# A two-branch streaming encoder layer: weight sums moved to VectorE, lag-kernel copies to GpSimd, S5 runs and projection B's loads begun in the last projection pair

## Chip, cores and metric

One core of a Trainium2 chip. The metric is the device time of one launch in microseconds, the median over runs. The engines are called TensorE (PE in the profile), ScalarE (ACT), VectorE (DVE), GpSimd (POOL) and SyncE (SP).

## What is computed

One layer over 2048 prompt frames and 8 x 16 sample frames (2176 in all), model width 1024, all in float32:

```python
h = rmsnorm(x, ln_g)
u_a, z_a, u_b, z_b, g_a, g_b = split(h @ w_in)          # 512, 512, then 4 x 1024 columns
y_a = gelu(s5_mixer(u_a, ...))                          # 32 groups of 16 channels, 64 complex states each
y_a = y_a * sigmoid(y_a @ w_glu + b_glu)
p_a = (y_a * silu(z_a)) @ w_pa
y_b = rglru(causal_conv(u_b, ...), ...)                 # conv of width 4, gated linear recurrence
p_b = (y_b * silu(z_b)) @ w_pb
m   = sigmoid(g_a) * p_a + sigmoid(g_b) * p_b
out = x + m @ w_out                                     # then a final rmsnorm
```

It also returns the last states of the recurrences and of the conv.

## The kernel before

Every matrix product is done with float16 halves: an operand is a high part and a low part, and a product takes three matmuls (`passes`, L161 to L163: high by high, high by low, low by high). Frames go in tiles of 512 columns, the sample frames in one tile of 128.

The program's order on each engine is written by the kernel itself. Stages, in order of time:

- the norm and the S5 input projection; then four blocks of gate columns done directly;
- sixteen *pairs* (`run_pair`): each multiplies two blocks of 128 columns of `w_in` with all frames. A pair is two `quad`s of seven block products, one for frame tiles 0 and 1 and one for 2 and 3 (a Strassen-like scheme), with the sample tile between them: 15 positions, `pos` 1 to 7, 8, and 9 to 15. Pairs alternate between branch B columns ("b") and gate columns. The last pair is of the kind "za";
- projection B: `p_b` tile by tile (n = 0 to 4, eight blocks m each), beside which the S5 runs go;
- the GLU, the projection of branch A and the merge, then the output projection.

**Weights of a pair.** `w_forms` makes the scheme's eight weight forms from the four blocks A11, A12, A21, A22. Four are sums of blocks, each computed by one `gtt` (GpSimd `tensor_tensor`, L56) into `wt` (`t`) or in place into `wraw` (A21). `high` (ScalarE) then makes the float16 high part, `low` (VectorE) the low part. `tt` is the same operation on VectorE (L53). The eight steps run beside the pair before, one a position, and each yields the cost that it charges.

**Background work.** After each product, `hook` calls `pump` with a budget (2.8 less what the position itself costs). `pump` lets `tasks` and then `low` go on until the budget is used up. `tasks` holds the conv and recurrence work of branch B (`b_work`, one task for two tiles) and the S5 runs; `low` holds `w_spill` (44 weight blocks split and written to DRAM, 16 of them for `w_pb`) and two `s5_prep` generators. `busy(NO_SPILL)` and `busy(NO_PREP)` stop these at some places of a pair: `place` is 0 + `pos` in a "b" pair and 15 + `pos` in a gate pair.

**S5.** `s5_prep` makes, for each of the 16 pairs of groups q, an input matrix `wb`, an output matrix `wc` (products on GpSimd, L56) and a kernel of lags. The last one goes through DRAM (`kpD`), comes back as `dd`, and `lags` copies it into another order (`d2`, ScalarE, two activations for a q) and stores it into `sD`. `s5_run(q)` loads `sD[q]` into one of four pages of the tag `t1` (L1415), `u` and `etD`, waits seven clocks, and then takes some six steps on TensorE, ScalarE and VectorE, with temporary tiles from one page `temp`. Four runs at most are in flight. `tail_start` waits for all runs and all spills, then loads `wo` and prepares the GLU's input: `ya` is read back (L1588), split into `yh` (ScalarE and VectorE).

**The last pair.** `hook_z` takes the place of the plain hook. At positions 8 to 11 it loads the four `wpb` pages (tag `t0`, which holds frame sums of the first quad until then), at 9 it calls `s5_open`, at 13 `y_load(0)`, branch B's output of tile 0. `y_load` first pumps until the tile's last block has been handed to its store. All these DMAs go through SyncE's queue, in program order with the loads of spill blocks (L1157) and of `dd` (L1293). The S5 runs are put into `tasks` only after this pair.

Of the kernel before, what the change touches and what calls it, by code (L numbers as in the profile page):

```python
# [8 lines left out]
F32 = mybir.dt.float32  # L9
# [4 lines left out]
MUL, ADD, SUB, MAX, MIN = ALU.mult, ALU.add, ALU.subtract, ALU.max, ALU.min  # L14
# [3 lines left out]
P = 128  # L18
# [29 lines left out]
def build(tc, I, O):  # L48
    nc = tc.nc
    V, S, G, PE, SP = nc.vector, nc.scalar, nc.gpsimd, nc.tensor, nc.sync  # L50

    def tt(out, a, b, op):
        V.tensor_tensor(out=out, in0=a, in1=b, op=op)  # L53

    def gtt(out, a, b, op):
        G.tensor_tensor(out=out, in0=a, in1=b, op=op)  # L56
# [19 lines left out]
    def scopy(out, a, scale=1.0):  # L76
        act(out, a, AF.Copy, scale=scale)

    with ExitStack() as es:
# [108 lines left out]
        pga = es.enter_context(tc.tile_pool(name="pga", bufs=1))  # L188
# [8 lines left out]
        hs = pga.tile([P, KB, 2, P], F16, name="hs")  # L197
# [17 lines left out]
        with ExitStack() as p1x:  # L215
# [328 lines left out]
            for n in range(4):  # L544
# [8 lines left out]
                for m in range(4):  # L553
                    p = proj(lambda k: wua[m][:, k], n)
# [33 lines left out]
                    if n == 3:  # L588
                        SP.dma_start(out=uD[1024 * m:1024 * m + 1024].rearrange("(p t) x -> p (t x)", t=8),
                                     in_=uE[m].rearrange("p t l j c -> p (t l j c)"))  # L590
# [10 lines left out]
        def page_b(tag, shape, name, dt=F16):  # L601
            return pgb.tile([P] + list(shape), dt, tag=tag, name=name, bufs=4)
# [6 lines left out]
        def gt(shape, dt=F32, name="g"):  # L609
            return gp.tile(list(shape), dt, tag="g", name=name, bufs=slots)  # L610
# [49 lines left out]
        tasks = []  # L660
        low = []
        branch_b = True
        clock = 0
# [109 lines left out]
        def w_forms(raw, W):  # L773

            r1, r2 = raw
            A11, A12, A21, A22 = r1[:, 0:4], r1[:, 4:8], r2[:, 0:4], r2[:, 4:8]
            t = wp.tile([P, 4, P], F32, tag="wt", name="wt", bufs=1)
            for h in range(2):
                W[h] = None

            def high(nm, src):
                h, i = FORMS[nm]
                if W[h] is None:
                    W[h] = w_half()
                scopy(W[h][:, i, :, 0], src, WS)

            def low(nm, src):
                h, i = FORMS[nm]
                stt(W[h][:, i, :, 1], src, WS, W[h][:, i, :, 0], MUL, SUB)

            high("A11", A11)
            gtt(t, A21, A22, ADD)
            yield 0.1
            low("A11", A11)
            high("S1", t)
            yield 0.7
            low("S1", t)
            gtt(t, t, A11, SUB)
            high("A12", A12)
            yield 0.7  # L800
            low("A12", A12)
            high("S2", t)
            yield 0.7
            low("S2", t)
            gtt(t, A12, t, SUB)
            yield 0.7
            high("A21", A21)
            high("S4", t)
            yield 0.2
            low("A21", A21)  # L810
            gtt(A21, A11, A21, SUB)
            low("S4", t)
            yield 1.4
            high("S3", A21)
            high("A22", A22)
            yield 0.2
            low("S3", A21)
            low("A22", A22)
            yield 1.3
# [304 lines left out]
        prepared = set()  # L1124

        place = 0

        def busy(no):

            return branch_b and place in no  # L1130

        NO_SPILL = range(13, 22)
        NO_PREP = range(11, 22)

        def w_spill():
# [49 lines left out]


        todo = list(range(16))
        temp = None

        def scratch(nm):  # L1190

            if nm == "w":
                return temp[:, 512:1024].rearrange("p (a r c) -> p a r c", a=2, r=2)
            return temp[:, 1024:1280].rearrange("p (r c) -> p r c", r=2)

        def s5_prep(second):

            def lags(q, dd):
                d2 = gt([P, 2, 4, P], F16, name="d2")
                for j in range(2):  # L1200
                    scopy(d2[:, j].rearrange("p a (h t) -> p a h t", t=8),
                          dd.rearrange("p g l (j t h) -> p j (g l) h t", j=2, t=8)[:, j])
                G.dma_start(out=sD[q, :, 2], in_=d2.rearrange("p j a x -> p (j a x)"))
                prepared.add(q)

            dd = None
            while second and not prepared:
                yield Later(1)
            while todo:
# [4 lines left out]
                q = todo.pop(0)  # L1214
# [30 lines left out]
                p = ps("a", (P, 4, P))  # L1245
# [22 lines left out]
                for g in range(2):  # L1268
# [3 lines left out]
                    for j in range(2):  # L1272
                        w = P - 16 * j
                        PE.matmul(o[:, 16 + P * j:16 + P * j + w], lhsT=lb,
                                  rhs=wc[:, j, g].rearrange("p (h t) -> p t h", t=8)[:, 0:w // 16],
                                  start=True, stop=True)
# [12 lines left out]
                dd = q, gt([P, 2, 2, 256], F16, name="dd")  # L1289
                for g in range(2):  # L1290
                    for l in range(2):
                        kk = kpD[q, g, :, l, 128:384]
                        SP.dma_start(out=dd[1][:, g, l],  # L1293
                                     in_=bass.AP(kk.tensor, kk.offset, [list(kk.ap[0]), [-16, 8], list(kk.ap[1])]))
# [39 lines left out]
        for n in range(NT):  # L1334
            if n == 1:
                load_states()
            for i in range(2):
                direct(2 + i, n, lambda k: W1[2 * i + k // 4][:, k % 4])
                if n < NT - 1:
                    c = next(wg) if n > 1 else 0  # L1340
# [65 lines left out]
        running = 0  # L1406

        def s5_run(q):
            nonlocal running
            while q not in prepared or running > 3:  # L1410
                yield Later(1)
            running += 1
            page = page_b("t1", (2048,), "sp", F32)
            sp, ph = page[:, 0:1536].bitcast(F16).rearrange("p (a x) -> p a x", a=3), page[:, 1536:1792]
            SP.dma_start(out=sp, in_=sD[q])  # L1415
            u = gt([P, 2, 2, 2, NC], F16, name="u")
# [1 line left out]
                         in_=uD[256 * q:256 * q + 256].rearrange("(g p) x -> p g x", g=2))  # L1418
# [4 lines left out]
            dd = sp[:, 2].rearrange("p (j a x) -> p j a x", j=2, a=4)  # L1423
# [9 lines left out]
            n = P  # L1433
            er, ei = (ph[:, o:o + n][:, None, :].to_broadcast([P, 2, n]) for o in (0, P))
            m16_ = m16c[:, q:q + 1].to_broadcast([P, n])
            w, hs_ = scratch("w"), scratch("hs")
            tt(w[:, 0], v[:, :, 0:n], er, MUL)
            tt(w[:, 1], v[:, :, 0:n], ei, MUL)
            tt(hs_[:, 0], w[:, 0, 0], w[:, 1, 1], ADD)
# [28 lines left out]
            for g in range(2):  # L1468
                p = ps("b")[:, 0:272]
                pj = [p[:, 0:NC], p[:, NC:272]]  # L1470
                uf = [u[:, g, b].rearrange("p j c -> p (j c)") for b in range(2)]
                PE.matmul(p, lhsT=dd[:, 0, 2 * g], rhs=uf[0], start=True, stop=False)
                PE.matmul(p, lhsT=dd[:, 0, 2 * g], rhs=uf[1], start=False, stop=False)
                for a, b in pas:
                    PE.matmul(pj[1], lhsT=dd[:, 1, 2 * g + a], rhs=u[:, g, b, 0], start=False, stop=False)
                for j in range(2):
                    for a, b in pas:
                        PE.matmul(pj[j], lhsT=wcs[:, a, j, g], rhs=hst[:, g, b], start=False, stop=False)
                PE.matmul(p, lhsT=dd[:, 0, 2 * g + 1], rhs=uf[0], start=False, stop=True)  # L1479
                sc = 1.0 / (VS * WCS)  # L1480
                act(yo[:, g, 0:256].rearrange("p (n j c) -> p j n c", n=4, j=2),
                    p.rearrange("p (j c) -> p j c", j=2)[:, :, 0:P].rearrange("p j (n c) -> p j n c", n=4),
                    AF.Gelu_apprx_tanh, scale=sc)
                act(yo[:, g, 256:272].rearrange("p (j c) -> p j c", j=2),
                    p.rearrange("p (j c) -> p j c", j=2)[:, :, P:NC], AF.Gelu_apprx_tanh, scale=sc)
                r0 = 256 * q + 128 * g
                G.dma_start(out=yDp[:, r0:r0 + P].rearrange("n p x -> p n x"),
                            in_=yo[:, g, 0:256].rearrange("p (n x) -> p n x", n=4))
                G.dma_start(out=yDs[r0:r0 + P], in_=yo[:, g, 256:272])
                running -= g  # L1490
                yield Step(0.6)


# [62 lines left out]
        def y_load(n):  # L1556
            while (7, n) not in stored:
                beside()
            for h in range(2):
                if n < NT - 1:  # L1560
                    Y[n, h] = page_load(page_a("h", (4, 2, 512), "Y"),
                                        ybD[n, 4 * h:4 * h + 4].rearrange("k p l t -> p k l t"))
                else:
                    Y[n, h] = page_load(hs[:, 4 * h:4 * h + 4], ybS[4 * h:4 * h + 4].rearrange("k p l t -> p k l t"))

        def hook_z(pos, c):
            nonlocal clock
            clock += 1
            pump(2.8 - c)
            if pos == 7:  # L1570
                while done["spill"] < 16:
                    clock += 1
                    pump(1e9)
            if 7 < pos < 12:
                wpb_load()
            if pos == 9:
                s5_open()
            if pos == 13:
                y_load(0)

        run_pair(15, hook_z)
        branch_b = False
        temp = pga.tile([P, 2048], F32, tag="w", name="temp", bufs=3)
        s5_init()
        def ya_load(m, n):
            if n < NT - 1:
# [45 lines left out]
            for _ in chain(glu_prep(0), glu_prep(1)):  # L1632
                yield Step(1.4)

        for q in range(16):
            tasks.append([clock + 3 * q, s5_run(q)])
        tasks.append([clock, tail_start()])

        def load_w(dst, src):
# [20 lines left out]
        for n in range(NT):  # L1660
            w = TILES[n][1]
            for m in range(8):
# [4 lines left out]
                p = ps("mm")[:, :w]  # L1667
# [196 lines left out]
```

## Time and profile before

| | us |
|---|---|
| median of 3 runs (lowest to highest) | 1551.13 (1546.92 to 1555.46) |
| the profiled execution's own time | 1549.53 |
| its span | 1547.7 |
| TensorE busy | 1446.3 (93%) |
| VectorE busy | 1034.2 (67%) |
| ScalarE busy | 815.5 (53%) |
| GpSimd busy | 505.3 (33%) |

The span runs from the first to the last instruction of the profiled execution; the time of that execution is 1.8 us longer. TensorE's busy time counts matmuls that overlap, so it is not time at the peak rate. The sixteen pairs lie between 230.4 and 983.75 us of the span, projection B between 983.75 and 1213.7, the GLU, the projection of branch A and the first output products up to 1284.

### The profile page before, as it was taken

What the parts mean: (1) busy time and instruction counts of PE and PEld (TensorE: products, weight loads), DVE (VectorE), ACT (ScalarE), POOL (GpSimd) and SP (SyncE); (2) the same over time, 40 slices, a digit from 0 to 9 for tenths busy, and PEclk for the clock granted to TensorE, in tenths of its full rate; (3) what the DMA queues carried; (4) which work ended last, traced back from release to release, by engine and by line L of the source; (5) the groups of instructions that cost most, each with busy time, mean ns of one, the idle gap of its engine ahead of it and who ended that gap; (6) DMA issues with size and microseconds to landing.
All of it is one profiled execution on the core that took longest, in us unless ns stands there. A gap on an engine that the chain in (4) does not pass through costs nothing.

```text
span 1547.7 us, 22800 instructions
## 1 busy us (share of the span) xinstructions
PE 1446.3 (93%) x8168; PEld 724.0 (47%) x8168; DVE 1034.2 (67%) x1913; ACT 815.5 (53%) x1526; POOL 505.3 (33%) x781
## 2 busy tenths in 40 slices
PE   7999999999899999998898899799999899999998
PEld 4544445444444444444443444355555544454444
DVE  5546768867588686887768777444445696665543
ACT  7642446757577575874856758423222562542322
POOL 0790133444536444274363642223332200000000
PEclk9999999999999999999999999899999899999999
DMA  8325223332423424241333241998766772163521
GB/s 207 106 92 208 89 77 93 102 122 86 140 82 109 130 86 140 76 158 61 104 127 92 87 134 69 324 360 292 251 214 221 265 255 72 70 219 107 177 82 55
DMA packets 168490, 222.21 MB, mean 144 GB/s; under 512 B 39258, under 2 KB 117738, under 8 KB 166328
## 3 DMA queue, kind: packets, MB, share of 16 engines
q1 hardware_dynamic: 144440, 150.96, 30.8%
q0 software_dynamic: 23936, 69.79, 12.0%
q8 instruction: 64, 1.05, 0.3%
q14 instruction: 50, 0.41, 0.1%
HBM read 133.85 MB, written 86.84 MB: 143 GB/s over the span
## 4 chain that ended last, share of the span: by engine, by line
PE 48%; issue 15%; DVE 11%; POOL 10%; ACT 7%; DMA 7%; SPq 2%; POOLq 0%; DVEq 0%; ACTq 0%
PE ps_mm L161 11%; PE ps_mm L163 11%; PE ps_mm L162 11%; PE ps_mm L1773 4%; PE ps_mm L1771 4%; PE ps_mm L1772 4%; DVE xc L65 2%; POOL wt L56 2%; POOL t L56 2%; POOL wc L56 1%; POOL wb L56 1%; DVE wf L65 1%; ACT L74 1%; POOL wraw L56 1%; ACT d L74 1%
## 5 line engine op out<-in xcount | busy, mean ns | idle before, releaser
L161 PE MATMUL ps_mm<-T,wf 128*128 128x512 f16 x512 | 198.8, 388 | 34.8 <-ACT gs L74 23.0
L163 PE MATMUL ps_mm<-T,wf 128*128 128x512 f16 x512 | 198.7, 388 | 1.3 <-DVE wf L65 1.3
L162 PE MATMUL ps_mm<-T,wf 128*128 128x512 f16 x512 | 198.6, 388 | 0.0
L162 PEld LDWEIGHTS <-wf 128*128 128x128 f16 x1232 | 121.7, 99 | 151.3 <-issue 46.2
L161 PEld LDWEIGHTS <-wf 128*128 128x128 f16 x1232 | 121.8, 99 | 121.6 <-issue 12.0
L163 PEld LDWEIGHTS <-wf 128*128 128x128 f16 x1232 | 121.7, 99 | 119.9 <-issue 7.0
L161 PE MATMUL ps_mm<-h,wf 128*128 128x512 f16 x448 | 171.2, 382 | 2.0 <-ACT wf L74 2.0
L163 PE MATMUL ps_mm<-h,wf 128*128 128x512 f16 x448 | 170.8, 381 | 0.7 <-DVE wf L65 0.7
L162 PE MATMUL ps_mm<-h,wf 128*128 128x512 f16 x448 | 170.8, 381 | 0.0
L161 PE MATMUL ps_mm<-Y,wpb 128*128 128x512 f16 x256 | 98.0, 383 | 11.0 <-DMA Y<-ybD 11.0
L65 DVE SCALAR_TENSOR_TENSOR gb<-gb,ps_mm 128x512 f32<-128x512 f32 (+1 forms) x40 | 24.3, 607 | 115.3 <-PE ps_mm L163 115.3
L1773 PE MATMUL ps_mm<-wo,M 128*128 128x512 f16 (+2 forms) x264 | 98.0, 373 | 3.4 <-DVE M L65 3.4
L1771 PE MATMUL ps_mm<-wo,M 128*128 128x512 f16 (+2 forms) x264 | 98.0, 373 | 0.0
L1772 PE MATMUL ps_mm<-wo,M 128*128 128x512 f16 (+2 forms) x264 | 98.0, 373 | 0.0
L162 PE MATMUL ps_mm<-Y,wpb 128*128 128x512 f16 x256 | 98.0, 383 | 0.0
L163 PE MATMUL ps_mm<-Y,wpb 128*128 128x512 f16 x256 | 97.8, 382 | 0.0
L74 ACT ACT_TABLE_LOAD x64 | 82.1, 1283 | 3.7 <-PE ps_mm L163 1.8
L65 DVE SCALAR_TENSOR_TENSOR xc<-ub,PC,xc 128x512 f32<-128x512 f32 x96 | 79.9, 832 | 3.2 <-ACT xc L74 1.0
L65 DVE SCALAR_TENSOR_TENSOR wf<-wraw,wf 128x512 f16<-128x512 f32 (+1 forms) x82 | 64.8, 806 | 6.2 <-ACT wf L74 6.1
L65 DVE SCALAR_TENSOR_TENSOR xo<-ps_mm,xo 128x512 f32<-128x512 f32 (+2 forms) x35 | 23.6, 674 | 65.4 <-PE ps_mm L1773 65.4
L1065 POOL DMA_DIRECT2D gbD<-gs x40 | 21.8, 546 | 134.4 <-ACT gs L74 134.3
L74 ACT ACTIVATE yo<-ps_a 128x256 f32<-128x256 f32 x64 | 14.7, 281 | 86.1 <-PE ps_a L1479 86.0
(323 smaller groups left out, 3529.2 us busy)
## 6 DMA issues: line engine op xcount, KB each, us to landing
wraw<-w_in SPq DMA_DIRECT2D x38, 512.0 KB, 4.4
sp<-sD SPq DMA_DIRECT2D x16, 768.0 KB, 4.9
xt<-x_prompt SPq DMA_DIRECT2D x16, 512.0 KB, 4.2
gbD<-gs POOLq DMA_DIRECT2D x32, 256.0 KB, 2.3
ybD<-y POOLq DMA_DIRECT2D x32, 256.0 KB, 2.8
gaD<-gs POOLq DMA_DIRECT2D x32, 256.0 KB, 2.5
Y<-ybD SPq DMA_DIRECT2D x8, 1024.0 KB, 9.9
gb<-gbD SPq DMA_DIRECT2D x32, 256.0 KB, 6.9
```

The source lines that it names most:

```text
L56: G.tensor_tensor(out=out, in0=a, in1=b, op=op)
L65: V.scalar_tensor_tensor(out=out, in0=a, scalar=s, in1=b, op0=op0, op1=op1)
L74: S.activation(out=out, in_=a, func=f, **kw)
L161: PE.matmul(p, lhsT=a[:, 0], rhs=b[:, 0], start=first, stop=False, skip_group_check=more)
L162: PE.matmul(p, lhsT=a[:, 0], rhs=b[:, 1], start=False, stop=False, skip_group_check=more)
L163: PE.matmul(p, lhsT=a[:, 1], rhs=b[:, 0], start=False, stop=last, skip_group_check=more)
L1065: G.dma_start(out=dst[m, :, t0:t0 + w], in_=t)
L1771: PE.matmul(p, lhsT=lh[0], rhs=w_[:, 0, c], start=(k == 0), stop=False)
L1772: PE.matmul(p, lhsT=lh[0], rhs=w_[:, 1, c], start=False, stop=False)
L1773: PE.matmul(p, lhsT=lh[1], rhs=w_[:, 0, c], start=False, stop=(k == KB - 1))
```

## The change

Four things are changed.

1. In `w_forms` the four sums go from GpSimd to VectorE, and the yields after them grow by 0.6 each (2.4 in all for a pair).
2. `lags` copies with GpSimd instead of ScalarE.
3. The last pair: `wpb` pages are loaded at positions 2, 3, 5 and 7, `y_load(0)` comes at 8, and the S5 runs are put into `tasks` at position 9 (the first starts two clocks later, the next ones at 3, 5, 7 and then every two clocks). From position 7 on preparation stays stopped (`closing`). The places at which spilling stops change from 13 to 21 to 15 to 20.
4. Runs 4, 5 and 6 take their page from the tag `w` (three pages) and do not count towards the four, so that up to seven are in flight. `temp` is gone, and each run has its own temporary tiles.

```diff
             high("A11", A11)
-            gtt(t, A21, A22, ADD)
-            yield 0.1
+            tt(t, A21, A22, ADD)
+            yield 0.7
...
-            gtt(t, t, A11, SUB)
+            tt(t, t, A11, SUB)
             high("A12", A12)
-            yield 0.7
+            yield 1.3
...
-            gtt(t, A12, t, SUB)
-            yield 0.7
+            tt(t, A12, t, SUB)
+            yield 1.3
...
-            gtt(A21, A11, A21, SUB)
+            tt(A21, A11, A21, SUB)
             low("S4", t)
-            yield 1.4
+            yield 2.0
...
-            return branch_b and place in no
-
-        NO_SPILL = range(13, 22)
+            return branch_b and ((closing and no is NO_PREP) or place in no)
+
+        NO_SPILL = range(15, 21)
...
-                    scopy(d2[:, j].rearrange("p a (h t) -> p a h t", t=8),
-                          dd.rearrange("p g l (j t h) -> p j (g l) h t", j=2, t=8)[:, j])
+                    G.tensor_copy(out=d2[:, j].rearrange("p a (h t) -> p a h t", t=8),
+                                  in_=dd.rearrange("p g l (j t h) -> p j (g l) h t", j=2, t=8)[:, j])
...
-            while q not in prepared or running > 3:
+            other = 4 <= q < 7
+            while q not in prepared or (running > 3 and not other):
                 yield Later(1)
-            running += 1
-            page = page_b("t1", (2048,), "sp", F32)
+            if other:
+                page = pga.tile([P, 2048], F32, tag="w", name="sp", bufs=3)
+            else:
+                running += 1
+                page = page_b("t1", (2048,), "sp", F32)
...
-            w, hs_ = scratch("w"), scratch("hs")
+            w, hs_ = gt([P, 2, 2, P], name="hw"), gt([P, 2, P], name="hs")
...
         def hook_z(pos, c):
-            nonlocal clock
+            nonlocal clock, closing
+            closing = 6 < pos
...
-            if pos == 7:
+            if pos == 2:
                 while done["spill"] < 16:
...
-            if 7 < pos < 12:
+            if pos in (2, 3, 5, 7):
                 wpb_load()
             if pos == 9:
                 s5_open()
-            if pos == 13:
+            if pos == 8:
                 y_load(0)
+            if pos == 9:
+                start = [clock + 2, clock + 3, clock + 5, clock + 7]
+                for q in range(16):
+                    tasks.append([start[q] if q < 4 else start[3] + 2 * (q - 3), s5_run(q)])
...
-        temp = pga.tile([P, 2048], F32, tag="w", name="temp", bufs=3)
...
-        for q in range(16):
-            tasks.append([clock + 3 * q, s5_run(q)])
```

## Rows read from the trace of the kernel before

**Rows 1.** Busy time by engine in the pairs, projection B and the GLU part.

```profile
core 0: us, PE busy (x) PEld busy (x) DVE busy (x) ACT busy (x) POOL busy (x), PEclk, DMA share, GB/s
230.40:983.75 753.35, 701.54 (x3903) 343.64 (x3902) 569.21 (x862) 507.93 (x889) 344.86 (x445) 0.98 0.34 110
983.75:1213.70 229.95, 218.95 (x1542) 124.67 (x1541) 105.04 (x331) 62.26 (x190) 73.46 (x121) 0.98 0.79 272
1213.70:1284.00 70.30, 58.03 (x248) 24.43 (x246) 66.49 (x103) 43.45 (x56) 1.58 (x3) 0.90 0.70 237
```

**Rows 2.** Waits of TensorE in the pairs: total, times, longest, in us.

```profile
PE ps_mm L161 <- ACT gs L74: 23.0, 11, 5.8
PE ps_mm L161 <- ACT ub L74: 10.3, 7, 3.5
PE ps_a L162 <- DVE xs L53: 7.3, 4, 4.3
```

**Rows 3.** Seven half-clock stretches in the pairs, summed; then the two later ones.

```profile
sum 34.12, PE 28.25 PEld 10.36 DVE 19.33 ACT 29.44 POOL 21.25; mean PE 4.04 PEld 1.48 DVE 2.76 ACT 4.21 POOL 3.04
...
987.62:997.86 10.24, 4.55 (x11) 1.62 (x11) 1.75 (x3) 2.14 (x2) 2.35 (x4) 0.50 0.94 319
1216.31:1229.96 13.65, 8.86 (x19) 2.46 (x19) 12.85 (x12) 13.27 (x14) 0.00 (x0) 0.50 0.95 323
```

**Rows 4.** Timeline around 380 to 392 us, GpSimd, ScalarE, TensorE: start, length.

```profile
380.12 1.59 POOL L56 TENSOR_TENSOR wc<-wc,t 128x512 f32<-128x512 f32 x1
...
382.79 1.27 POOL L56 TENSOR_TENSOR wt<-wraw 128x512 f32<-128x512 f32 x1
...
384.10 0.63 ACT L74 ACTIVATE wf<-wt 128x512 f16<-128x512 f32 x1 [4.87 <-POOL wt L56]
...
389.05 2.11 ACT L74 ACTIVATE d<-dd 128x512 f16<-128x512 f16 x2
...
391.70 0.58 PE L161 MATMUL ps_mm<-T,wf 128*128 128x512 f16 x1 [5.83 <-ACT gs L74]
```

**Rows 5.** Waits of ScalarE in the pairs: total, times, longest.

```profile
ACT wf L74 <- POOL wt L56: 48.7, 27, 4.9
```

**Rows 6.** GpSimd in the pairs, slowest and fastest sum: count, busy us, mean ns.

```profile
L56 POOL TENSOR_TENSOR wt<-wt,wraw 128x512 f32<-128x512 f32 x15 | 23.6, 1570 | 26.2 <-DVE wf L65 26.2
...
L56 POOL TENSOR_TENSOR wt<-wraw 128x512 f32<-128x512 f32 x15 | 19.8, 1321 | 14.2 <-DMA wraw<-w_in 14.1
```

**Rows 7.** The widest copy on GpSimd, from the preparation before the pairs.

```profile
L434 POOL COPY pw<-stk x1: 299/299/299, 73.8 to 73.8; 128x64 f32<-128x64 f32 x1
```

**Rows 8.** VectorE by line in the pairs: one operand in PSUM, then both in SBUF.

```profile
L53 DVE TENSOR_TENSOR gs<-ps_mm,gs 128x512 f32<-128x512 f32 x48 | 32.8, 684 | 16.7 <-PE ps_mm L163 16.4
...
L65 DVE SCALAR_TENSOR_TENSOR q<-q,xc 128x512 f32<-128x512 f32 x32 | 28.7, 897 | 0.3 <-ACT q L74 0.2
```

**Rows 9.** Timeline at 714 us, VectorE and GpSimd.

```profile
713.95 5.59 DVE L65 SCALAR_TENSOR_TENSOR xc<-ub,PC,xc 128x512 f32<-128x512 f32 x3
...
714.10 1.25 POOL L56 TENSOR_TENSOR wc<-par 128x256 f32<-128x256 f32 x2
```

**Rows 10.** SyncE's queue around the end of the last pair.

```profile
983.86 2.46 SPq L1293 DMA_DIRECT2D dd<-kpD  x4
986.37 1.14 SPq L1545 DMA_DIRECT2D Y<-ybD  x2
```

**Rows 11.** Waits of TensorE after the pairs.

```profile
PE ps_mm L161 <- DMA Y<-ybD: 11.0, 2, 9.3
PE ps_mm L161 <- ACT yh L74: 4.4, 2, 3.9
```

**Rows 12.** S5 runs' page loads (first and last start), and the GLU input's read-back.

```profile
L1415 SPq DMA_DIRECT2D sp<-sD x16: 319/320/1577, 989.0 to 1162.2; - x16
...
1207.61 10.69 SPq L1588 DMA_DIRECT2D ya<-yDp  x8
```

**Rows 13.** VectorE's low parts of the GLU input, min/median/max ns.

```profile
L53 DVE TENSOR_TENSOR yh<-ya,yh x32: 426/1273/1486, 1216.7 to 1281.5; 128x256 f16<-128x256 f32 x24, 128x64 f16<-128x64 f32 x8
```

More of the change, by code (lines that the diff above doesn't have):

```diff
@@ L1126, in build @@
         place = 0
+        closing = False
         def busy(no):
-            return branch_b and place in no
-        NO_SPILL = range(13, 22)
+            return branch_b and ((closing and no is NO_PREP) or place in no)
+        NO_SPILL = range(15, 21)
         NO_PREP = range(11, 22)
@@ L1187, in build @@
         todo = list(range(16))
[L1188 to L1194, printed above, removed]
         def s5_prep(second):
@@ L1489, in s5_run @@
                 G.dma_start(out=yDs[r0:r0 + P], in_=yo[:, g, 256:272])
-                running -= g
+                running -= 0 if other else g
                 yield Step(0.6)
```

## The prediction

> **What bounds the kernel now.** First the windows by stage, to see whether TensorE is ever short of work [rows 1]. It is the bound nearly everywhere, and what can be won is its idle time and its time at half clock. In the sixteen pairs it is busy 701.5 of 753.4 us, so it is idle 51.8 us. In projection B it is idle 11.0 us, in the GLU part 12.3 of 70.3 us. Then TensorE's waits. In the pairs 33.3 us are waits for a ScalarE eviction (23.0 for the gate snaps, 10.3 for the branch B ones), 7.3 us for VectorE [rows 2]. In B the idle time is one wait, for the first Y tile, 11.0 us [rows 11]. Third the granted clock. It falls to 0.50 (1.2 of 2.4 GHz) behind long waits: in seven stretches of the pairs, 34.1 us in all, with TensorE busy 28.3; once behind the Y wait, 10.2 us, busy 4.6; once in the GLU part, 13.7 us, busy 8.9 [rows 3]. Work at half clock takes twice its time, so half of those busy sums is lost: 14, 2.3 and 4.4 us.
>
> Why ScalarE is late is seen in one timeline [rows 4]. A product for the next PSUM bank waits 5.83 us for a snap. ScalarE had stood 4.87 us for GpSimd's first sum of weights, which was queued on GpSimd behind a product of the S5 preparation (`wc`, begun at 380.12), and it then spent 2.11 us on two lag copies right ahead of that snap. Without these 6.98 us there is no wait. In all, ScalarE waits 48.7 us for such sums in the pairs [rows 5].
>
> **Sums on VectorE.** 15 pairs with four sums, 60 in this stretch. On GpSimd one takes 1.32 to 1.57 us, 60 x 1.45 = 87 us [rows 6]. On VectorE a two-operand operation on 128x512 float32 takes 0.684 us when nothing holds it up [rows 8], so 60 x 0.684 = 41 us are added to 569 busy of 753 (76%) [rows 1]: 81% if nothing is given back. Something is: an operation with both operands in SBUF takes 0.897 us in the mean, one with an operand in PSUM 0.684 [rows 8], and three `xc` steps take 5.59 us while GpSimd works [rows 9]. Bounds for what 87 us of GpSimd work take from VectorE: nothing, and all 87. This form alone loses 32 x 0.213 = 6.8 us, and it is one of many. I take about half of the 87, 40, so the move is neutral for VectorE's sum. What the edit removes is ScalarE's wait, 48.7 us. The grown yields take 15 x 2.4 = 36 units from background work; that work ends in time anyway, since preparation and spill have B as a reserve.
>
> **Lag copies.** 32 copies of 1.05 us (2.11 / 2) leave ScalarE [rows 4], 30 of them in the pairs: 32 us. On GpSimd no copy of this size is in the trace. The bounds are 0.30 us, a copy of 64 columns [rows 7], and 1.57 us, the slowest two-input sum of 512 [rows 6]. It is nearest to the sums in size, so I take 1.3 us: 39 us, less than half of the 87 that leave. What is queued behind a copy there are the store of `sD` and the next `wc` products.
>
> The Trainium skill (SBUF — State Buffer, "Who interferes with whom") says that a VectorE instruction with two SBUF inputs contends with a GpSimd instruction that reads SBUF, and that the second to issue blocks fully. The rows agree (0.897 against 0.684 us, and 5.59 us for three). By that rule the copies, which read SBUF, hold VectorE up as the sums did.
>
> Sum for the pairs: of 33.3 us of eviction waits I take two thirds, 22, and of the 14 us of clock loss 8. Against that, VectorE now makes the sums in order behind `b_work`, and ScalarE can wait there. I charge 8 us, about what it costs today that VectorE is late (7.3) [rows 2]. Net **-22 us**. Bounds: all of the waits and the clock gone, -47; every sum on the path, 60 x 0.684 = +41.
>
> **Y and `wpb` early.** The load of Y is ready to go before the end of the pair, but in SyncE's queue it stands behind four `dd` loads that go at 983.86; Y goes at 986.37 [rows 10]. With preparation stopped there are no `dd` loads ahead of it, and five positions of 753.4 / 16 / 15 = 3.1 us lie between 13 and 8. Ahead of it may still be a spill load that waits for a free tile, and the store of the last `b_work` of tile 0. Wait and clock are 11.0 + 2.3 = 13.3 us; I leave 2: **-11 us** (0 to -13).
>
> **S5 early, seven in flight.** The runs' loads begin at 989.0, the last at 1162.2 [rows 12]: 173 us for 15 steps, four in flight, so four rounds of some 46 us. The GLU's input is read back at 1207.6, with B's end at 1213.7: all of its copies are late. VectorE needs 16 low parts of 1.27 us for the first two tiles, 20 us [rows 13], and is busy 66.5 of 70.3 us there [rows 1]. Now run 0 starts four positions before the pair's end, and three runs of the first seven need no page of the four. Runs 0 to 3, 7 to 10, 11 to 14 and 15 are what queues for the four pages, so the last run begins at 3 x 46 = 138 us after the first instead of 173, and the first some 10 us earlier: the runs end about 45 us earlier. Read-back (10.7 us of issues) and 20 us of copies fit into that. VectorE is busy 105 of 230 us in B and ScalarE 62 [rows 1], so the copies are hidden there; were VectorE as full as in the pairs, those 20 us would come back. Idle time and clock of the GLU part are 12.3 + 4.4 = 16.7 us; I take **-14 us** (0 to -17). The denser runs can make TensorE wait in B now and then: **+2** (0 to 6).
>
> **Sum.** -22 - 11 - 14 + 2 = -45. Against the profiled execution's own 1549.53 us that is 1504.5. The median of the runs is 1.6 us above that execution, so the time is **1506 us**.
>
> **Rivals.**
> - *The lag copies cost VectorE what the sums gave back.* 39 us of GpSimd copies, each holding VectorE for its whole length, put VectorE at 569 + 41 + 39 - 40 = 609 of 753, and ScalarE waits for sums that come late. The pairs then win half: 1506 + 11 = 1517. For it: [rows 9]. Against: half of the ScalarE time is freed whatever VectorE does. Chance 0.18. The rule of the Trainium skill named above is this rival's mechanism.
> - *The S5 runs end early, but the GLU's start does not move.* `tail_start` waits for all spills too, and spills are in `low`, which starves while seven runs use up the budget. Then the 14 us stay: 1520. For it: runs and spills share 2.5 units a clock. Against: after the first seven only four are in flight, as now. Chance 0.14.
> - *Transfers hidden badly.* Spill loads and page waits in SyncE's queue hold Y, and the GLU stays late: only the pairs win, 1506 + 11 + 14 = 1531. Chance 0.09.
> - *VectorE becomes the bound of the pairs (slower).* Place: the positions in which `taps` and `scan` of `b_work` are queued ahead of a sum; ScalarE stands behind it, and the snaps behind ScalarE. Price 0.684 us a sum. It ends above before from the point at which the pairs lose more than the 23 us that the ends win, that is 34 of 60 sums wholly on the path with none of the old waits gone; with all 60 it is 1551 + 41 - 23 = 1569. Against: VectorE has a quarter of its time free. Chance 0.07, and 0.07 more for a loss in the pairs that just eats the 23 us, 1551.
> - *Nearly all idle time goes:* -40 in the pairs, -13, -17: 1481. Chance 0.08.
>
> My forecast has 0.37. Range: from 1484, which leaves the last rival out, to 1536, beyond the third: 0.78 is inside. Half a per cent, 8 us, is about what a measurement of this kernel can tell. Faster by more than that: 0.86 (all but the slower cases); within it 0.07; slower 0.07.
>
> **What will show it.** ScalarE's wait for GpSimd's sums is gone from the pairs, with no wait of like size for VectorE in its place; TensorE's eviction waits there are near 11 us. The half-clock stretches in the pairs are three or fewer. GpSimd's copies show about 1.3 us. Y is issued before 975 us on the old scale, and TensorE goes from the last pair into B without a gap of 3 us. The last S5 page is loaded 45 us earlier, and `yh` is written before the GLU starts. I would be wrong if ScalarE waits for VectorE's sums for more than 25 us, if the copies take over 2.5 us, or if the read-back of the GLU input still stands at the end of B.

## The result and the profile after

The changed kernel takes 1510.37 us (median of four, 1505.42 to 1512.01) against 1551.02 for the kernel before; the ratio is 0.9732, 95% interval 0.9697 to 0.9767. The forecast was 1506 in 1484 to 1536. The profiled execution took 1509.87 us with a span of 1508.1, 39.6 less than before.

Where it came from is not what the sum said. In this table of the two profiles the pairs are counted from the first sample-tile product of the first pair to the last product of the last pair, B from there to its last matmul (with the wait for Y), the GLU part from there to the first output product. The windows of [rows 1] have slightly other ends:

| us | up to the pairs | pairs | B | GLU part | rest | span |
|---|---|---|---|---|---|---|
| before | 237.7 | 745.9 | 230.3 | 61.1 | 272.9 | 1547.7 |
| after | 240.2 | 709.0 | 226.5 | 58.0 | 274.5 | 1508.1 |
| difference | +2.5 | -36.9 | -3.8 | -3.1 | +1.6 | -39.6 |

The windows by stage of the changed kernel, in the columns of [rows 1]:

```profile
232.90:949.30 716.40, 690.70 (x3874) 340.21 (x3873) 567.60 (x911) 475.96 (x851) 265.33 (x385) 0.99 0.36 118
949.30:1175.60 226.30, 221.76 (x1570) 126.49 (x1569) 112.98 (x342) 66.41 (x200) 97.51 (x153) 0.99 0.78 274
1175.60:1242.60 67.00, 56.20 (x247) 24.18 (x245) 66.17 (x103) 42.05 (x55) 1.59 (x3) 0.95 0.69 236
```

TensorE's idle time in the pairs falls from 51.8 to 716.4 - 690.7 = 25.7 us. VectorE's busy time does not move (567.6 against 569.2), though 60 sums were added; which parts of the change add up to that is seen further down. In the GLU part VectorE is as full as before, 66.2 of 67.0 us.

TensorE's waits in the pairs of the changed kernel, to be read against [rows 2]:

```profile
PE ps_a L162 <- DVE xs L53: 7.7, 3, 3.7
PE ps_mm L161 <- DVE gs L53: 7.1, 3, 4.2
PE ps_mm L161 <- ACT gs L74: 4.0, 1, 4.0
...
PE ps_mm L161 <- ACT ub L74: 0.2, 1, 0.2
```

The eviction waits are down from 33.3 to 4.2 us; in their place stand 7.1 us for VectorE's gate sums. The half-clock stretches of the pairs, summed, against the first of [rows 3]:

```profile
sum 17.00, PE 15.39 PEld 5.43 DVE 14.93 ACT 12.92 POOL 2.48; mean PE 3.85 PEld 1.36 DVE 3.73 ACT 3.23 POOL 0.62
```

Four stretches instead of seven, 17 us instead of 34. The prediction wanted three or fewer. ScalarE's wait for the sums in the pairs, against [rows 5], and then GpSimd's lag copy, against the bounds in [rows 6, 7]:

```profile
ACT wf L74 <- DVE wt L53: 19.0, 16, 3.8
```

```profile
L1194 POOL COPY d<-dd x32: 1097/1115/1586, 310.7 to 1118.1; 128x512 f16<-128x512 f16 x32
```

ScalarE waits 19.0 us for VectorE's sums instead of 48.7 for GpSimd's. SyncE's queue before the end of the last pair (949.2), against [rows 10]:

```profile
929.86 2.48 SPq L1286 DMA_DIRECT2D dd<-kpD  x4
...
933.01 0.98 SPq L1542 DMA_DIRECT2D Y<-ybD  x2
```

Y goes 16 us before the pair's end instead of 3 us behind it, and the wait for Y [rows 11] is gone. What is left behind the pairs, TensorE's waits first, then the S5 page loads (first and last start) and the read-back in SyncE's queue, against [rows 12]:

```profile
PE ps_mm L162 <- DVE yh L53: 4.4, 4, 1.3
PE ps_a L1469 <- ACT yo L74: 3.5, 1, 3.5
```

```profile
L1412 SPq DMA_DIRECT2D sp<-sD x16: 319/438/1422, 935.4 to 1121.8; - x16
```

```profile
1167.25 1.49 SPq L1589 DMA_DIRECT2D ya<-yDp  x3
```

The first page load comes 14 us before the pairs' end instead of 5 us behind it, but the last one still 173 us behind it (before: 179), and the read-back still stands at B's end, 8 us ahead of it. That is one of the three signs by which the prediction said it would be wrong, and most of the S5 part of the forecast did not happen.

### The profile page after: what moved, and what is told of

It is laid out like the page before. It is cut to its first block, busy times and chain, and to the rows that moved or that the text cites. A ratio compares the mean times of both kernels' runs of the same rounds, so it can differ in the third digit from the quotient of the medians.

```text
span 1508.1 us, 22745 instructions
## 1 busy us (share of the span) xinstructions
PE 1440.5 (96%) x8168; PEld 725.2 (48%) x8168; DVE 1041.0 (69%) x1977; ACT 786.2 (52%) x1494; POOL 443.4 (29%) x749
## 4 chain that ended last, share of the span: by engine, by line
PE 68%; DVE 13%; issue 7%; ACT 5%; DMA 4%; POOL 2%; SPq 1%; DVEq 0%; POOLq 0%; ACTq 0%
PE ps_mm L161 17%; PE ps_mm L163 17%; PE ps_mm L162 17%; PE ps_mm L1772 4%; PE ps_mm L1771 4%; PE ps_mm L1770 4%; DVE yh L53 2%; DVE wf L65 2%; DVE xc L65 1%; ACT L74 1%; DMA wraw<-w_in 1%; PE ps_a L172 1%; DMA xt<-x_prompt 1%; PE ps_a L1475 1%; PE ps_a L1267 1%
## 5 line engine op out<-in xcount | busy, mean ns | idle before, releaser
L161 PE MATMUL ps_mm<-T,wf 128*128 128x512 f16 x512 | 196.7, 384 | 11.9 <-DVE gs L53 7.1
L163 PE MATMUL ps_mm<-T,wf 128*128 128x512 f16 x512 | 196.5, 384 | 1.5 <-DVE wf L65 1.5
L162 PE MATMUL ps_mm<-T,wf 128*128 128x512 f16 x512 | 196.3, 383 | 0.0
L65 DVE SCALAR_TENSOR_TENSOR xc<-ub,PC,xc 128x512 f32<-128x512 f32 x96 | 74.7, 778 | 2.3
L74 ACT ACTIVATE gs<-ps_mm 128x512 f32<-128x512 f32 (+1 forms) x92 | 48.3, 534 | 29.8 <-PE ps_mm L163 27.1
L1065 POOL DMA_DIRECT2D gbD<-gs x40 | 21.7, 544 | 141.6 <-ACT gs L74 141.6
```

The lines of the kernel that those rows point to most:

```text
L65: V.scalar_tensor_tensor(out=out, in0=a, scalar=s, in1=b, op0=op0, op1=op1)
L74: S.activation(out=out, in_=a, func=f, **kw)
L161: PE.matmul(p, lhsT=a[:, 0], rhs=b[:, 0], start=first, stop=False, skip_group_check=more)
L162: PE.matmul(p, lhsT=a[:, 0], rhs=b[:, 1], start=False, stop=False, skip_group_check=more)
L163: PE.matmul(p, lhsT=a[:, 1], rhs=b[:, 0], start=False, stop=last, skip_group_check=more)
L1065: G.dma_start(out=dst[m, :, t0:t0 + w], in_=t)
```

## The experiments

Profiles of one and the same order of work differ too: through the pairs the changed kernel and three of the kernels below (`e5_front`, `e10_budget`, `e11_four`) hold the same work in the same order but for its very end, and their pairs take 709.0, 714.6, 715.7 and 713.6 us. Differences of pairs under 7 us are not read, and of these four the changed kernel's 709.0 is the shortest. In this table the stages of a kernel are those of one execution, its profiled one, and the ratio is of all its executions; kernels whose intervals overlap are not told apart by their time:

| us | pairs | B | GLU part | last S5 page load behind the pairs | ratio to before, 95% |
|---|---|---|---|---|---|
| before | 745.9 | 230.3 | 61.1 | 178.8 | 1 |
| after | 709.0 | 226.5 | 58.0 | 172.8 | 0.9732 (0.9697 to 0.9767) |
| e1_sums | 724.2 | 234.6 | 70.9 | 183.2 | 0.9992 (0.9966 to 1.0019) |
| e2_lags | 754.2 | 231.5 | 60.4 | 180.1 | 1.0044 (1.0028 to 1.0060) |
| e3_end | 745.4 | 218.0 | 54.7 | 157.6 | 0.9865 (0.9825 to 0.9904) |
| e4_sums_old_cost | 735.5 | 230.7 | 61.5 | 179.2 | 0.9906 (0.9876 to 0.9937) |
| e5_front | 714.6 | 221.7 | 64.5 | 177.5 | 0.9763 (0.9747 to 0.9779) |
| e6_prep_on | 716.8 | 225.4 | 54.5 | 165.0 | 0.9747 (0.9733 to 0.9762) |
| e7_old_cost | 743.5 | 218.0 | 54.6 | 157.6 | 0.9853 (0.9836 to 0.9869) |
| e8_lags_act | 708.1 | 225.3 | 58.0 | 174.7 | 0.9726 (0.9711 to 0.9740) |
| e9_gpsimd_sums_paced | 718.8 | 222.9 | 58.0 | 169.3 | 0.9755 (0.9729 to 0.9780) |
| e10_budget | 715.7 | 230.8 | 47.1 | 146.1 | 0.9691 (0.9670 to 0.9713) |
| e11_four | 713.6 | 219.6 | 60.1 | 163.0 | 0.9701 (0.9675 to 0.9727) |
| e12_all | 707.5 | 220.6 | 47.1 | 140.7 | 0.9613 (0.9596 to 0.9629) |

### The parts alone

**The sums alone, with their grown yields** (`e1_sums`):

```diff
-            gtt(t, A21, A22, ADD)
-            yield 0.1
+            tt(t, A21, A22, ADD)
+            yield 0.7
...
```

and so on for the four sums, as in the change.

> The kernel before with the four weight sums on VectorE and the grown yields, nothing else. In the changed kernel the pairs are about 37 us shorter. My theory: ScalarE's 48.7 us of waiting for GpSimd's sums is the main cause, so this part alone takes 20 to 28 us off the pairs and nothing off projection B or the GLU part: 1524 to 1532 us. Rival, work moved out of the pairs (three preparations that now end in B): this part alone gives under 12 us, 1540 us or more. Rival, VectorE as the bound: slower than 1551.

None of the three: the pairs got 21.7 us shorter, as my theory said, and the time stayed the same (1554.93 us, ratio 0.9992). TensorE's waits from 950 us on say where it went:

```profile
PE ps_mm L161 <- ACT yh L74: 14.3, 1, 14.3
PE ps_mm L161 <- DMA Y<-ybD: 12.6, 2, 10.1
```

The grown yields leave less budget for background work. By the end of the pairs 32 spilled blocks were stored instead of 37 and 14 lag kernels instead of 15. The rest runs beside B, together with the S5 runs. The last spilled block, for which `tail_start` waits, is stored 238 us behind the pairs instead of 141, the GLU's input is read back behind B's end, and the GLU part begins 14.3 us late. In the profiled execution, the fastest of ten (1545.15 us), 14 of the 21.7 us come back in B and the GLU part; over all executions nothing is won.

**The same sums with the old yields** (`e4_sums_old_cost`; `gtt` to `tt` alone):

```diff
-            gtt(t, A21, A22, ADD)
+            tt(t, A21, A22, ADD)
             yield 0.1
...
```

> The sums on VectorE with the old, smaller yields, so that the background work gets its old budget. If the gain comes from GpSimd's queue alone, this is within 5 us of the kernel with sums and grown yields. If it comes from background work held back (2.4 units a pair, 36 in all), this loses 10 us or more of that kernel's gain. If VectorE is close to its limit in the pairs, waits of ScalarE for VectorE grow here.

14 us faster than the kernel with grown yields (0.9906 against 0.9992), with pairs that are 11 us longer: B and the GLU part are as before. So in the kernel before, holding back background work was a bad trade, and moving the sums by itself a gain of 10 us in the pairs. TensorE's waits there, against [rows 2]:

```profile
PE ps_a L162 <- DVE xs L53: 19.1, 5, 5.3
PE ps_mm L161 <- ACT ub L74: 8.4, 6, 2.3
PE ps_mm L161 <- ACT gs L74: 5.3, 10, 2.2
```

The eviction waits fall from 33.3 to 13.7 us, as my forecast had it, but the wait for VectorE's `xs` grows from 7.3 to 19.1 and takes more than half of it back. VectorE's busy time in the pairs is 567.5 us with 60 sums more, against 565.9: for the sums alone, GpSimd gave back what they cost.

**The lag copies alone** (`e2_lags`):

```diff
-                    scopy(d2[:, j].rearrange("p a (h t) -> p a h t", t=8),
...
+                    G.tensor_copy(out=d2[:, j].rearrange("p a (h t) -> p a h t", t=8),
...
```

> The kernel before with the lag copies on GpSimd, nothing else. My theory: 32 us of ScalarE time are freed, some evictions come 2 us earlier, but the sums on GpSimd wait behind copies of 1.1 us: 3 to 10 us faster, 1541 to 1548 us. Rival, the copies hold up VectorE and the sums' queue: no change or slower, 1549 us or more, with ScalarE's wait for GpSimd's sums above 60 us.

Slower, as the rival said. The pairs of the kernel before, then of this one, in the columns of [rows 1], and this one's ScalarE wait:

```profile
237.70:983.60 745.90, 694.09 (x3866) 339.93 (x3865) 565.92 (x856) 506.81 (x887) 344.13 (x444) 0.98 0.34 110
```

```profile
241.50:995.60 754.10, 698.86 (x3865) 340.86 (x3864) 598.42 (x856) 477.49 (x857) 376.86 (x474) 0.97 0.33 109
```

```profile
ACT wf L74 <- POOL wt L56: 66.3, 32, 4.9
```

The time is 1560.30 us. GpSimd works 32.7 us more and VectorE is busy 32.5 us longer with the same 856 instructions. The two sums are alike, as if the copies held VectorE for their whole length; no single copy was followed. ScalarE's wait for GpSimd's sums grows from 48.7 to 66.3 us, and yet TensorE's eviction waits fall to 26.0 us (20.1 and 5.9); other waits of TensorE grew.

**The last pair and the S5 runs alone** (`e3_end`: the change without its first two parts).

> The changed kernel with sums on GpSimd and lag copies on ScalarE as before, so the new last pair, the early S5 runs and the seven in flight alone. My theory: the Y wait and its half clock go (13 us), the pairs stay within 5 us, the GLU part gains 3 us as it does in the changed kernel: 1533 to 1540 us. Rival, work moved out of the pairs: the pairs get 10 us or more shorter here too and the time is under 1530. Rival, the late preparations eat what Y wins: 1545 or more.

As my theory said, 1533.34 us; the pairs are unchanged (745.4). B is 12.3 us shorter (9.5 of it the gap ahead of its first product) and the GLU part 6.4. Both gains are larger than in the changed kernel, where they are 3.8 and 3.1: the first two parts take some of it back, and by the next kernel it is the grown yields that do.

### What makes the pairs shorter

**All of the change with the old yields** (`e7_old_cost`):

```diff
             tt(t, A21, A22, ADD)
-            yield 0.7
+            yield 0.1
```

and likewise 1.3 to 0.7, 1.3 to 0.7, 2.0 to 1.4.

> The changed kernel with the old, smaller yields after the sums. The sums alone took 21.7 us off the pairs with grown yields and gave 14 us back behind them, and took 10.4 us off with the old ones and gave nothing back. My theory: the same trade here. The pairs are some 10 us longer than in the changed kernel (719), B and the GLU part together 10 to 14 us shorter: 1505 to 1511 us. Rival, the grown yields only delay: pairs as short as now and the ends shorter, under 1502. Rival, VectorE falls behind in the pairs: over 1515.

The trade is there, but steeper, and the time, 1529.17 us, is the second rival's: the pairs take 743.5 us, hardly less than before, although the sums and the lag copies are where the change puts them. The ends are those of `e3_end`. The eviction waits are down here too, to 10.8 us (6.6 and 4.2). But VectorE falls behind: TensorE waits 9.0 us for its gate sums, and its largest wait in the pairs is this one:

```profile
PE ps_a L162 <- DVE xs L53: 18.2, 5, 4.0
```

**The lag copies on ScalarE again** (`e8_lags_act`, the reverse of `e2_lags` in the changed kernel).

> The changed kernel with the lag copies on ScalarE again. Alone, with the sums on GpSimd, the copies on GpSimd cost 8 us in the pairs. The pairs of the changed kernel are 15 us shorter than those of the sums alone. If that is the lag copies (with the sums gone GpSimd has room for them, and evictions are no longer behind them on ScalarE), the pairs here are 720 to 727 us and the time 1519 to 1528. If it is that preparation is stopped in the last pair, the pairs stay within 5 us of 709 and the time within 5 us of 1510.

No difference in time (1510.06) or in the pairs (708.1). With the sums gone from GpSimd, the copies cost and win no time. They still cost VectorE: its 905 instructions in the pairs are busy 543.4 us here and 564.2 (904) in the changed kernel, 20.8 us more beside 26 copies that keep GpSimd busy 30.2 us. That is two thirds of their length, where `e2_lags` had all of it.

**The sums on GpSimd again, grown yields kept** (`e9_gpsimd_sums_paced`); the order of work on TensorE, ScalarE and SyncE is then that of the changed kernel instruction by instruction:

```diff
-            tt(t, A21, A22, ADD)
+            gtt(t, A21, A22, ADD)
             yield 0.7
```

and so for all four.

> The changed kernel with its grown yields but the sums back on GpSimd. Pair by pair, the long pairs of the kernel before (51 to 54 us) are those in which both preparations begin at once; with the grown yields they begin one a pair and most pairs take 43 to 44 us; with the old yields and the sums on VectorE the long pairs are back. New theory, pacing: the grown yields spread the preparations, and the engine of the sums is worth little: pairs within 12 us of 709, time 1508 to 1524. Rival, the engine of the sums (my forecast's theory): ScalarE waits for GpSimd's sums 40 us or more again, pairs 730 us or more, time 1530 or more.

By its numbers the pacing theory holds: 1515.48 us, pairs 718.8. My forecast's theory, that ScalarE's wait for the sums is what makes the pairs long, falls by these waits in its pairs, ScalarE's first and then TensorE's:

```profile
ACT wf L74 <- POOL wt L56: 67.7, 29, 6.3
```

```profile
PE ps_mm L161 <- ACT gs L74: 5.8, 2, 3.4
PE ps_mm L161 <- ACT ub L74: 4.9, 3, 3.8
```

ScalarE waits for GpSimd's sums longer than in the kernel before (67.7 against 48.7 us), and yet TensorE waits for evictions only 10.7 us instead of 33.3. What this kernel has and `e3_end` has not is the grown yields and the lag copies on GpSimd; its pairs are 26.6 us shorter. With the sums on GpSimd, the copies alone made the pairs 8 us longer (`e2_lags`), so the shorter pairs are the yields' doing. The grown yields with sums on GpSimd and copies on ScalarE were not run. That one preparation a pair instead of two at once is the reason, as the expectation has it, was not tested by itself, and the trace of the kernel before does not bear it out: a pair in which two preparations begin takes 46.0 us (from 470.7 us), one with a single one 53.8 (from 754.4).

### What holds the S5 runs

**Preparation and spill ahead of the runs** (`e5_front`):

```diff
         run_pair(15, hook_z)
         branch_b = False
+        tasks[:0] = low
+        low.clear()
```

> The changed kernel, with preparation and spill put ahead of the S5 runs once the last pair is over. In the changed kernel three lag kernels reach DRAM 95 to 170 us after the pairs, and the last S5 page is loaded 172.8 us after them. My theory: preparation starves behind seven runs for pump budget. Put in front, the last page load comes 15 to 30 us earlier, the GLU part is 8 to 12 us shorter, and the time is 1496 to 1504. Rival, projection B's transfers or VectorE set the pace of the runs: the last page load stays within 5 us, and the time within 4 us of 1510.

The order alone does not do it: the last load is 5 us later and the GLU part 6.5 us longer, 1514.89 us. What preparation gains the runs lose: the three lag kernels go to DRAM 37 to 78 us behind the pairs instead of 97 to 170.

**Preparation not stopped in the last pair** (`e6_prep_on`):

```diff
-            return branch_b and ((closing and no is NO_PREP) or place in no)
+            return branch_b and (place in no)
```

> The changed kernel without the stop of preparation from position 7 of the last pair on. If stopping it is what makes the last preparations late, fewer are left for B and the GLU part gets 3 to 8 us shorter, 1502 to 1508 us. If its loads get ahead of Y in SyncE's queue, as in the kernel before, TensorE waits up to 9 us at the end of the pairs and the time is 1512 to 1520.

The GLU part is 3.5 us shorter, and 5.8 us pass between the last product of the pairs and the first of B. But that is not the expected wait for Y: Y goes at 938.72, 17 us before the pairs' end, behind four `dd` loads as in the changed kernel. TensorE waits there for a product of the preparation itself:

```profile
PE ps_a L172 <- POOL wb L56: 4.3, 1, 4.3
```

1513.29 us, no difference that the intervals can tell.

**Four runs in flight instead of seven** (`e11_four`):

```diff
-            other = 4 <= q < 7
+            other = False
```

> The changed kernel with four runs in flight and none on the pages of the other tag. If three more in flight are what brings the runs' end forward, the last S5 page load comes 15 us or more later and the GLU part gets 8 us or more longer: 1518 or more. If the budget holds the runs, nothing changes by more than 4 us: 1506 to 1514.

1507.43 us, no difference that the intervals can tell. The three runs on the other pages bring nothing; without them the last load even comes 10 us earlier and B is 6.9 us shorter.

**A larger budget beside B** (`e10_budget`):

```diff
             clock += 1
-            pump(2.5)
+            pump(3.5)
```

> The changed kernel with a budget of 3.5 instead of 2.5 for each call beside projection B. Theory: the S5 runs, with three preparations and eight spills left over, are held by that budget (16 x 6.9 + 3 x 3.6 + 8 units, 129, at 2.5 a clock are 52 clocks), not by VectorE, which is half idle there. The last S5 page load comes 20 us or more earlier, the GLU part is 4 to 10 us shorter, time 1499 to 1506. Rival, the runs are held by pages and the chain of a run: last load within 8 us, time within 4 us of 1510. Rival, TensorE then waits in B for runs that ScalarE or VectorE has not finished: B 5 us or more longer.

The budget is what held the runs: the last load comes 27 us earlier, and the GLU part is 47.1 us instead of 58.0. The time is 1505.22 us, with an interval that still touches the changed kernel's. Its TensorE waits behind the pairs hold none for `yh` any more, but two in the crowd of runs beside B, which is 4.3 us longer:

```profile
PE ps_a L1475 <- ACT hst L74: 4.8, 1, 4.8
PE ps_a L1424 <- ACT v L74: 2.3, 1, 2.3
```

**Budget, four runs, lag copies on ScalarE together** (`e12_all`; the three edits above).

> The changed kernel with a budget of 3.5 beside projection B, four runs in flight and the lag copies on ScalarE. The budget alone took 11 us off the GLU part and gave 4 back in B, where TensorE waited twice for ScalarE in a crowd of seven runs; four in flight alone had B 7 us shorter; the lag copies alone were worth nothing. Theory, these add: B near 222, the GLU part near 48, time 1497 to 1504. Rival, with four in flight the chain of a run is the limit and not the budget: the last S5 page load later than 155 us after the pairs, the GLU part 54 or more, time 1505 to 1510.

Better than expected: 1489.78 us (0.9613, 0.9596 to 0.9629), 20 us ahead of the changed kernel. B and the GLU part, in the columns of [rows 1]:

```profile
945.50:1166.10 220.60, 220.35 (x1572) 126.33 (x1571) 127.17 (x353) 87.65 (x218) 89.16 (x144) 1.00 0.87 302
1166.10:1213.20 47.10, 47.10 (x223) 21.57 (x221) 44.65 (x85) 26.41 (x40) 4.16 (x7) 1.00 0.70 224
```

TensorE is busy all the time in both, at a granted clock of 1.00. With four runs the two long waits of `e10_budget` do not come. The parts add up to 1502 us, and the three together are 12 us better than that. By the table B and the GLU part are 2 us better each than their parts add up to; the rest lies in the pairs and in what single executions differ by, and stays open.

## Why the prediction was right in the number and where its steps failed

**The pairs: right sign, half the mechanism.** Forecast -22, measured -36.9 (about -33 by the mean of the four profiles of one order). The failing step is under "Sums on VectorE": "What the edit removes is ScalarE's wait, 48.7 us", with the grown yields at nothing because the background work "ends in time anyway". `e7_old_cost` and the changed kernel differ in the yields alone, and their pairs take 743.5 and 709.0 us; in `e9_gpsimd_sums_paced` the wait stays, and grows, while the pairs get 26.6 us shorter than in `e3_end`. So the 36 units of budget that I priced at nothing are the larger term in the changed kernel, and the engine of the sums is worth some 5 us there at most (1515.48 against 1510.37, with intervals that overlap). The background work did not end in time either: `e1_sums` has it 14.3 us late.

What the forecast had right is that moved sums free evictions: alone they take these waits from 33.3 to 13.7 us (`e4_sums_old_cost`). What eats the gain is the term for a late VectorE, which I put at 8 us. TensorE's waits for `xs` and gate sums, 8.7 us before, are 21.1 there and 27.2 in `e7_old_cost`; only with the grown yields are they 14.8, so that 8 is about right.

The timeline of [rows 4] was read correctly, but one stall with two items ahead of it was taken for the rule. Even there ScalarE's wait ends at 384.10, before TensorE's begins (391.70 - 5.83 = 385.87); in the trace of the kernel before ScalarE is busy, not waiting, in 33.1 of the 33.3 us of eviction waits, 9.7 of them with lag copies. An account of the 36.9 us: 26.1 less idle time, about half of 28.3 - 15.4 = 12.9 us, 6.4, for the clock, and a remainder of 4 that fits work which left the pairs (14 `wcs` stores in them instead of 16). Why a smaller budget frees the evictions, that less background work then stands ahead of them on ScalarE and VectorE, is argued from these waits and not shown by a run of its own.

**VectorE neutral: right for the sums, and by two errors for the whole.** `e4_sums_old_cost` bears out the step that took about half of GpSimd's 87 us as given back (567.5 against 565.9 us with 60 more operations). That the changed kernel is neutral too is luck: the copies, by `e8_lags_act`, add 20.8 us, which the step leaves out, and the grown yields, from `e4_sums_old_cost` to `e1_sums` (539.1), take 28 off.

**Lag copies: the duration nearly right, the value nothing.** 1.12 us where I took 1.3. The first rival's mechanism is real: alone, the copies cost VectorE 32.5 us and the kernel 0.44%. That fits the rule of the Trainium skill (SBUF — State Buffer, "Who interferes with whom") that the later of the two blocks fully: 30 copies kept GpSimd busy 33.5 us. In the changed kernel they cost VectorE two thirds of their length, there is time for it, and it does not decide.

**Y: right in size, for another reason.** The gap between the pairs and B, 9.7 us, fell to 0.2; the 11.0 us that I called one wait were two, 9.3 and 1.7 us, and both are gone. I said that no `dd` loads would stand ahead of Y; four do, at 929.86. It is the positions that Y was moved forward by: `e6_prep_on` does not stop preparation, and Y goes 17 us before the end there too.

**S5: the step that failed by size.** I had the runs end 45 us earlier and the GLU part 14 us shorter; counted from the pairs' end, the last page load comes 6 us earlier, and the GLU part is 3.1 shorter. The first load does come 19 us earlier, but from the first to the last pass 186 us, where "four rounds of some 46 us" became three and 138. That took a run's length as fixed, although I had the budget of 2.5 in hand. With seven runs, three left-over preparations and the last spills beside B there is more work than budget, and the last run's page load (1121.8) follows the last lag copy (1118.1). The outcome is that of the second rival, given 0.14, and its shared budget is the cause, but not the spills it named: the last of them is stored at 1158.1, the last run's output at 1167.0, and the read-back begins at 1167.25. `e10_budget` confirms it (GLU part 47.1), and `e3_end`, in which only one preparation is left over, has the last load 15 us earlier than the changed kernel. B as a whole is 3.8 us shorter, where -11 for Y and +2 for denser runs make -9: without the gap of 9.7 it is 5.7 us longer, 3.5 of it a wait for `yo`.

**The sum** came out within 4.4 us by luck. Against the forecast the pairs won 15 us more, the GLU part 11 and B 5 less, and 4 us were lost ahead of the pairs and behind the GLU part, for which the sum had no term.

## What to carry to other kernels

In a schedule written by hand, a cost that is charged is as real an edit as an instruction: price it by the work that it moves, and look where that work lands, since the part alone may win 21.7 us in one stage and no time in all. Before putting more tasks in flight, add up their cost against the budget that feeds them. When a long wait of a helper engine is removed in thought, ask whether the bounding engine's wait ends with it: in `e9_gpsimd_sums_paced` one grew by 19 us while the other fell by 23.

## What was not expected of the hardware

A float16 copy of 128x512 in a changed order takes the same on GpSimd (1.115 us) as on ScalarE (1.127 us, 32.2 us for 30). Moving 30 of them to GpSimd lengthened VectorE's 856 instructions by 32.5 us (`e2_lags`), as much as GpSimd's own time for them; with the sums gone from GpSimd, 26 of them (30.2 us) lengthened VectorE's work by 20.8 us. So the copies were not free for VectorE in either kernel, and they did not cost it the same share of their time in both; why is not shown.
